# Ordering the small time-mixing work of a two-layer encoder: one chain of 36 steps per pair, a new pair every 8 slots

## The chip, the cores and the metric

The kernel runs on one core of one Trainium2 chip. TensorE (PE) multiplies, with its weight loads (PEld) overlapped; VectorE (DVE), ScalarE (ACT) and GpSimd (POOL) do elementwise work; SyncE (SP) issues the transfers. The metric is the device time of one execution in microseconds, smaller is better.

## The reference

The program is a two-layer encoder over 256 tokens of width 2048, in float32, batch 1. Layer 0 is RWKV-7 time mixing and a squared-ReLU MLP, layer 1 is chunked band attention and an MLP; every branch has an RMS norm and a shift, scale and gate computed from a vector `c` (the modulation). The change concerns the time mixing. Cut to what matters:

```python
xr, xw, xk, xv, xa, xg = [h + xx * mu[j] for j in range(6)]
r, k, v = xr @ w_r, xk @ w_k, xv @ w_v
w_log = -softplus(-(w0 + tanh(xw @ w1) @ w2)) - 0.5
a = sigmoid(a0 + (xa @ a1) @ a2)
g = sigmoid(xg @ g1) @ g2
kk = heads(k * k_k); kk = kk / norm(kk)
k = k * (1 + (a - 1) * k_a)
decay = exp(-exp(heads(w_log)))
def step(S, inp):                       # one token, 32 heads of 64x64 state
    sa = einsum('bhvk,bhk->bhv', S, -kk_t)
    S = S * w_t + sa[..., None] * (kk_t * a_t) + v_t[..., None] * k_t
    return S, einsum('bhvk,bhk->bhv', S, r_t)
y = group_norm(scan(step)) + sum(r * k * r_k) * v
return (y * g) @ w_o
```

## The kernel before, in words

Activations lie transposed: 128 channels (two heads, a *pair*) on the partitions, 256 tokens along the free axis, 16 pairs. Large products split each float32 operand into a high and a low part: a weight half of 128 x 1024 is fetched (`raw`), its high part is made by ScalarE (`wH`, line 371), the low one by VectorE (`wL`, line 374), and `proj2` multiplies each block of 128 rows twice, with 512 columns (line 405) and with 256 (line 406).

The scan is not run token by token but in four chunks of 64 tokens per pair. `Pair` holds it, as generators that yield at the end of every step. `early` (8 steps) makes decays, normalised keys and the scaled operands `kr`, `bh`, `kh`; `invert` (12 steps that do work) makes the 64 x 64 Gram matrices (PSUM tile `gr`) and inverts their triangular part by doubling, in 32 x 32 tiles (`iv`, `tt`, `xs`, `u`); `late` (16 steps) walks through the chunks. For each chunk c it forms `g` (read from PSUM by ScalarE), then `sa` (again ScalarE), then the state update, which VectorE adds to the old state as `zs` (lines 295 and 297). The three stand in the PSUM tile `chn`. The chunk's outputs are added up by further matmuls into the tile `py` (lines 283, 286, 301). After the chunks come the group norm, the gate and the product with `lg`.

Around the pairs, `proj_steps` makes k and r of a pair in 16 large steps of four matmuls (two blocks of rows each), and `out_steps` begins the output projection, in 44 large steps, once the last pair is projected. The modulation is summed on VectorE, one `raw` tile of 128 x 1024 per step (`ada`, lines 445 and 447).

The order: `layer_a` runs 19 periods of 16 slots. In period p, pair p is projected, pair p - 1 is in `early`, p - 2 in `invert`, p - 3 in `late`, each spread evenly over the 16 slots. In each slot the small steps are traced, then one large step; large work is queued on TensorE behind the small work of the slot before, and otherwise the scheduler of the language orders each engine's instructions from what it expects of readiness. `fin` gives out the column sums of the modulation a few at a time, and `ADA_SLOTS` names the slots with a modulation step. Each engine takes its instructions in the order so fixed.

PSUM has eight banks: two `pj` (large products), two `ms` (small ones), and one each of `gr`, `iv`, `chn` and `py`. `reuse_waits="tile"` pools make the next user of a buffer wait for the last readers of the old one. The lines on which the change turns:

```python
pch = pp.tile([P, 3, C], F32, tag="chn", bufs=1, name="chn")
nc.tensor.matmul(pch[K, 2, :], bk[K, 0, c, :], sa[K, :], start=False, stop=True)
nc.vector.scalar_tensor_tensor(out=zn, in0=zs, scalar=pc[:, c, :], in1=pch[:, 2, :], ...)
nc.tensor.matmul(ch(py)[K, c, :], sa[K, :], ch(ar)[K, c, :], start=False, stop=True)
```

Of the kernel before, what the change touches and what calls it, by code (L numbers as in the profile page):

```python
# [18 lines left out]
P = 128  # L19
D = 2048  # L20
T = 256
# [56 lines left out]
class Pair:  # L78

    EARLY = 8

    def __init__(self, body, j, v, tw, ta, tg, e01):
        self.b, self.j, self.v, self.tw, self.ta, self.tg, self.e01 = body, j, v, tw, ta, tg, e01
        self.heads = (slice(0, C), slice(C, P))

    def s(self, name="s", bufs=10):
        return self.b.pw.tile([P, T], F32, tag=name, bufs=bufs, name=name)
# [28 lines left out]
    def early(self):  # L118
# [27 lines left out]
        self.pc = pw.tile([P, 4, 1], F32, tag="pc", bufs=3, name="pc")  # L146
# [18 lines left out]
        kr = self.kr = self.big("kr", 3)  # L165
# [3 lines left out]
        rkp = s("rkp", 1)  # L169
# [4 lines left out]

        bk = self.bk = pw.tile([P, 3, 4, C], F32, tag="bk", bufs=3, name="bk")
        pt = b.psm().rearrange("p (a c k) -> p a c k", a=2, c=4)
        self.each(lambda c: pt[:, 0, c, :], lambda c: ch(v)[:, c, :], lambda c: cst("cen"))
        nc.scalar.copy(bk[:, 2], pt[:, 0])
# [5 lines left out]

    def invert(self):
        b, nc, s, ch, kr, bk, bh, kh = self.b, self.b.nc, self.s, self.ch, self.kr, self.bk, self.bh, self.kh
# [5 lines left out]
        def half(name, bufs):  # L192
            return b.pw.tile([P, 4, H], F32, tag=name, bufs=bufs, name=name)
# [10 lines left out]
        ar = self.ar = s("ar", 2)  # L204
# [20 lines left out]
        nc.scalar.copy(bk[:, 0:2], pt)  # L225
# [3 lines left out]
        for l in range(1, 6):  # L229
            tt_, xs = half("tt", 1), half("xs", 1)  # L230
            nc.vector.transpose(out=tt_.rearrange("p c t -> p (c t)"), in_=u.rearrange("p c t -> p (c t)"))
            pi = pp.tile([P, 16, H], F32, tag="iv", bufs=1, name="iv")[:, 0:4, :]
# [10 lines left out]
            pi = pp.tile([P, 16, H], F32, tag="iv", bufs=1, name="iv")[:, 0:4, :]  # L243
            if l < 5:
                self.tiles(pi, xs, u, [(i, i) for i in range(4)])
                nc.vector.tensor_tensor(out=u, in0=u, in1=pi, op=ALU.add)
            else:
                self.tiles(pi, xs, u, up)
                for K in QS[::2]:
                    nc.vector.tensor_copy(uf[K, :, H:C], pi[K])  # L250
            if l == 2:
                pg = pp.tile([P, 4, P], F32, tag="gr", bufs=1, name="gr")
                self.each(lambda c: pg[:, c, :], lambda c: ch(kh)[:, c, :], lambda c: kr[:, c, :])
                mk = self.mk = self.big("mk", 2)
                nc.vector.tensor_tensor(out=mk, in0=pg, in1=ui, op=ALU.mult)
            yield

    def late(self):
        b, nc, j, s, ch, v = self.b, self.b.nc, self.j, self.s, self.ch, self.v
        kr, ar, mk, bk, u, pc, heads = self.kr, self.ar, self.mk, self.bk, self.u, self.pc, self.heads  # L260
        pw, pp = b.pw, b.pp

        pyt = pp.tile([P, 2, T], F32, tag="py", bufs=1, name="py")
        py = pyt[:, 0, :]
        zs = None
        for c in range(4):
            if c == 1:
                lg = pw.tile([P, 2, P], F32, tag="lg", bufs=1, name="lg")
                nc.sync.dma_start(out=lg, in_=b.d["lora2"][j, :, 2:4])
            pch = pp.tile([P, 3, C], F32, tag="chn", bufs=1, name="chn")  # L270
            g, sa = (pw.tile([P, C], F32, tag=n_, bufs=2, name=n_) for n_ in ("g", "sa"))
            for K in heads:
                nc.tensor.matmul(pch[K, 0, :], mk[K, c, 0:C], bk[K, 2, c, :], start=True, stop=(c == 0))  # L273
            if c:
                for K in heads:
                    nc.tensor.matmul(pch[K, 0, :], kr[K, c, 0:C], zs[K, :], start=False, stop=True)
            nc.scalar.copy(g, pch[:, 0, :])
            yield
            for K in heads:
                nc.tensor.matmul(pch[K, 1, :], u[K, c, :], g[K, :], start=True, stop=True)  # L280
            nc.scalar.mul(sa, pch[:, 1, :], -1.0)
            for K in heads:
                nc.tensor.matmul(ch(py)[K, c, :], bk[K, 2, c, :], mk[K, c, C:P], start=True, stop=False)
            if c:
                for K in heads:
                    nc.tensor.matmul(ch(py)[K, c, :], zs[K, :], kr[K, c, C:P], start=False, stop=False)
            yield
            if c < 3:
                for K in heads:
                    nc.tensor.matmul(pch[K, 2, :], bk[K, 1, c, :], bk[K, 2, c, :], start=True, stop=False)  # L290
                for K in heads:
                    nc.tensor.matmul(pch[K, 2, :], bk[K, 0, c, :], sa[K, :], start=False, stop=True)
                zn = pw.tile([P, C], F32, tag="zs", bufs=2, name="zs")
                if c == 0:
                    nc.vector.tensor_copy(zn, pch[:, 2, :])
                else:
                    nc.vector.scalar_tensor_tensor(out=zn, in0=zs, scalar=pc[:, c, :], in1=pch[:, 2, :],
                                                   op0=ALU.mult, op1=ALU.add)
                zs = zn
            for K in heads:  # L300
                nc.tensor.matmul(ch(py)[K, c, :], sa[K, :], ch(ar)[K, c, :], start=False, stop=True)
            yield

        var, pg = pyt[:, 1, :], pyt[:, 1, :]
        sq = self.square(py)
        yield
        self.head_sums(var, sq)
        yield
        rg = s("sl", 2)
# [3 lines left out]
        yield  # L313
        for i in range(2):
            nc.tensor.matmul(pg, lg[:, i, :], self.tg[:, i, :], start=(i == 0), stop=(i == 1))  # L315
# [5 lines left out]
class Body:  # L321
    RAW_BUFS = 6
    W_BUFS = 3
    DRAIN_STEPS = (14, 14, 16)
    ADA_SLOTS = (1, 3, 6, 9, 11, 14)
    ADA_MORE = 10
# [296 lines left out]
    def layer_a(self, st, sp):  # L623
# [184 lines left out]
        with ExitStack() as s1:  # L808
# [12 lines left out]
            def proj_steps(pr):  # L821
                pr.lw = pw.tile([96, 2, P], F32, tag="lw", bufs=2, name="lw")
                nc.sync.dma_start(out=pr.lw, in_=d["lora2"][pr.j, :96, 0:2])
                for dst, hl in (("k", xk), ("r", xr)):
# [4 lines left out]
                    for kt in range(KT):  # L829
                        self.proj2(ps, w, lambda kt: hl[:, kt, :, 0:T], (kt, kt + 1))  # L830
                        if kt % 2 == 1:
# [7 lines left out]
            def out_steps():  # L839
# [3 lines left out]
                sums, todo = self.o_ps, [(n, 0, HK) for n in range(4)] + [(n, HK, KT - 2) for n in range(4)]  # L843
                for n, lo, hi in todo + [(n, 0, HK) for n in range(4, 8)]:
# [4 lines left out]
                    if lo == HK and n == 0:  # L849
                        for j in range(HK, KT - 2):  # L850
                            self.split(self.y_hl, j, v[:, j, :])
# [7 lines left out]
            stages = ((Pair.late, 16), (Pair.invert, 13), (Pair.early, Pair.EARLY), (None, 16))  # L859
            smalls, larges = [], []  # L860
            for p in range(NPAIR + 3):
                live = []
                if p == NPAIR:
                    self.y_hl = self.new_hl()
                    outs = out_steps()
                for i, (f, n) in enumerate(stages):
                    j = p - 3 + i
                    if 0 <= j < NPAIR:
                        live.append([proj_steps(pairs[j]) if f is None else f(pairs[j]), n, 0])
                if p >= NPAIR:  # L870
                    live.append([outs, self.DRAIN_STEPS[p - NPAIR], 0])
                dense = live.pop()
                for slot in range(16):

                    for gens, own, other, back in ((live, smalls, larges, 0), ([dense], larges, smalls, 2)):
                        with tc.issue_after(other[-back]) if back and len(other) >= back else nullcontext():
                            for g in gens:
                                while g[2] * 16 < g[1] * (slot + 1):
                                    next(g[0], None)
                                    g[2] += 1  # L880
                        own.append(self.last_pe())
                    self.lazy = True
                    self.fin(2)
                    if p >= 2 and (slot in self.ADA_SLOTS or slot == 7 and 3 <= p < 3 + self.ADA_MORE):
                        self.ada()
                    self.lazy = False
# [307 lines left out]
```

## Time and profile before

| | |
|---|---|
| median of 3 runs | 2713.09 us |
| lowest, highest | 2711.19, 2715.17 us |
| span of the profiled execution | 2707.4 us |
| between the span and the runs' times | 3.8 to 7.8 us (median 5.7) |
| pairs' stage, first large matmul to last small step | 210.3 to 750.3 us |
| TensorE busy, share of the span | 2645.1 us, 98% |
| VectorE busy | 2104.9 us, 78% |
| ScalarE busy | 1347.8 us, 50% |
| DMA, mean | 245 GB/s |

The profile is that of one execution; the page gives its span, from the first to the last instruction, and not its whole time, so sums are made against the span. A row of a group has the line, the engine, the operation, the tile written and the tiles read, the shapes and the count. A small float32 matmul shows twice in the trace, so "x4" in a row of a 64 x 64 product is one for each of the two heads. Matmuls are pipelined and their ends are modelled: times between two matmuls are best taken from start to start. "PE a <- DVE b" in the list of waits means that TensorE's instruction a stood idle until VectorE's b had ended.

### The profile page before, as it was taken

How to read it: one execution, taken by the hardware profiler on the slowest of the kernel's cores; microseconds unless marked ns; L12 is line 12 of the kernel's file. 1: busy time of each engine (PE TensorE's matmuls, PEld its weight loads, DVE VectorE, ACT ScalarE, POOL GpSimd, SP SyncE). 2: the span in 40 equal slices, each digit the busy share in tenths (PEclk: the TensorE clock that was granted, in tenths of full speed). 3: DMA queues.
4: the chain of work that ended last, by engine and by line, in shares of the span. 5: the costliest groups of instructions: out<-in, count | busy, mean ns of one | idle time of the engine just before them, and what ended most of it. 6: DMA issues, size and time to landing. Idle time of an engine off the chain costs nothing.

```text
span 2707.4 us, 58382 instructions
## 1 busy us (share of the span) xinstructions
PE 2645.1 (98%) x23690; PEld 2236.3 (83%) x23690; DVE 2104.9 (78%) x3109; ACT 1347.8 (50%) x2432; POOL 214.9 (8%) x320
## 2 busy tenths in 40 slices
PE   6999999999999999999999999999999999999997
PEld 3777777777888888888888898877898888888886
DVE  5778888888788788888888898899987555555555
ACT  3346444555355536445355554465565464453553
POOL 0002222322110000000000100000100000000002
PEclk9999999999999999999999999999999999999999
DMA  9966655665587789988889769887867555555553
GB/s 338 313 227 207 203 191 180 191 195 177 184 280 264 255 324 329 330 307 319 322 316 329 252 220 316 322 287 252 288 193 259 188 188 186 187 188 186 189 188 120
DMA packets 217390, 662.64 MB, mean 245 GB/s; under 512 B 21408, under 2 KB 68896, under 8 KB 217120
## 3 DMA queue, kind: packets, MB, share of 16 engines
q1 hardware_dynamic: 215056, 656.36, 71.7%
q8 instruction: 186, 3.05, 0.4%
q10 hardware_dynamic: 2064, 2.54, 0.3%
q14 instruction: 84, 0.69, 0.1%
HBM read 656.72 MB, written 2.10 MB: 243 GB/s over the span
## 4 chain that ended last, share of the span: by engine, by line
PE 91%; DVE 3%; issue 3%; ACT 1%; DMA 1%; POOL 1%; DVEq 0%; ACTq 0%; SPq 0%; POOLq 0%
PE pj L405 47%; PE pj L406 23%; PE iv L107 2%; PE pj L395 2%; PE pj L396 2%; PE pj L394 2%; PE gr L101 1%; PE o L394 1%; PE ms L101 1%; PE chn L273 1%; PE chn L280 1%; PE ms L111 1%; PE py L315 1%; DVE wL L374 1%; PE o L395 0%
## 5 line engine op out<-in xcount | busy, mean ns | idle before, releaser
L374 DVE TENSOR_TENSOR wL<-raw,wH 128x1024 fp32r<-128x1024 f32 x772 | 941.8, 1220 | 353.5 <-ACT wH L371 348.8
L405 PE MATMUL pj<-aHL,wH 128*128 128x512 f32 x3328 | 1214.3, 405 | 2.0 <-DVE x L914 1.1
L371 ACT CAST wH<-raw 128x1024 fp32r<-128x1024 f32 x772 | 805.9, 1045 | 796.6 <-PE pj L405 650.4
L406 PE MATMUL pj<-aHL,wL 128*128 128x256 f32 x3328 | 938.8, 282 | 0.0
L405 PEld LDWEIGHTS pj<-aHL,wH 128*128 128x128 f32 x3328 | 628.0, 189 | 154.4 <-issue 11.4
L405 PE MATMUL pj<-hHL,wH 128*128 128x512 f32 x2048 | 722.4, 398 | 0.0
L406 PEld LDWEIGHTS pj<-aHL,wL 128*128 128x128 f32 x3328 | 628.3, 189 | 3.9 <-issue 0.8
L406 PE MATMUL pj<-hHL,wL 128*128 128x256 f32 x2048 | 574.4, 281 | 0.0
L405 PEld LDWEIGHTS pj<-hHL,wH 128*128 128x128 f32 x2048 | 384.5, 188 | 93.8 <-DVE hHL L960 0.2
L406 PEld LDWEIGHTS pj<-hHL,wL 128*128 128x128 f32 x2048 | 386.8, 189 | 0.5 <-DVE wL L374 0.3
L447 DVE SCALAR_TENSOR_TENSOR acc<-rada,ct,acc 128x1024 f32<-128x1024 f32 x255 | 326.3, 1280 | 11.7 <-DMA rada<-w_ada 11.1
L511 POOL TENSOR_TENSOR ss<-ss,sq 128x256 f32<-128x256 f32 x56 | 54.8, 979 | 1587.1 <-ACT sq L510 1586.9
L985 DVE SCALAR_TENSOR_TENSOR x<-pj,mod,x 128x256 f32<-128x256 f32 x256 | 123.4, 482 | 58.4 <-PE pj L406 54.6
L447 DVE SCALAR_TENSOR_TENSOR acc<-raw,ct,acc 128x1024 f32<-128x1024 f32 x105 | 135.6, 1291 | 3.8 <-DMA raw<-w_ada 3.7
L396 PE MATMUL pj<-aHL,wL 128*128 128x258 f32 x384 | 108.6, 283 | 1.6 <-DVE wL L374 1.6
L957 ACT ACTIVATE t<-t 128x256 f32<-128x256 f32 x112 | 46.8, 418 | 126.9 <-DVE t L929 126.9
L395 PE MATMUL pj<-aHL,wH 128*128 128x258 f32 x384 | 109.6, 286 | 0.0
L394 PE MATMUL pj<-aHL,wH 128*128 128x258 f32 x384 | 109.5, 285 | 0.0
L396 PEld LDWEIGHTS pj<-aHL,wL 128*128 128x128 f32 x384 | 73.9, 193 | 1.9 <-DVE wL L374 1.8
L395 PEld LDWEIGHTS pj<-aHL,wH 128*128 128x128 f32 x384 | 73.3, 191 | 0.1
L394 PEld LDWEIGHTS pj<-aHL,wH 128*128 128x128 f32 x384 | 73.0, 190 | 0.2
L959 ACT ACTIVATE t<-t 128x256 f32<-128x256 f32 x128 | 53.4, 417 | 3.4
(244 smaller groups left out, 2846.6 us busy)
## 6 DMA issues: line engine op xcount, KB each, us to landing
raw<-w_up SPq DMA_DIRECT2D x256, 512.0 KB, 4.3
raw<-w_down SPq DMA_DIRECT2D x256, 512.0 KB, 4.2
rada<-w_ada SPq DMA_DIRECT2D x208, 512.0 KB, 5.7
raw<-w_ada SPq DMA_DIRECT2D x112, 512.0 KB, 4.4
rawa<-w_ada SPq DMA_DIRECT2D x64, 512.0 KB, 6.7
rada<-w_ada_kv SPq DMA_DIRECT2D x64, 512.0 KB, 6.2
raw<-w_k SPq DMA_DIRECT2D x32, 512.0 KB, 4.7
raw<-w_r SPq DMA_DIRECT2D x32, 512.0 KB, 4.7
```

The source lines that it names most:

```text
L101: self.b.nc.tensor.matmul(o(c)[K], lhsT(c)[K], rhs(c)[K], start=True, stop=True)
L107: self.b.nc.tensor.matmul(o[QS[K], c, :], lhsT[QS[R], c, :], rhs[QS[R], c, :], start=True, stop=True, tile_position=(H * R, H * K))
L371: nc.scalar.copy(Hf, raw)
L374: eng.tensor_tensor(out=Lf, in0=raw, in1=Hf, op=ALU.subtract)
L394: nc.tensor.matmul(ps, H[:, i, :], a(kt)[:, 0, :], start=(first and kt == 0), stop=False)
L395: nc.tensor.matmul(ps, H[:, i, :], a(kt)[:, 1, :], start=False, stop=False)
L396: ins = nc.tensor.matmul(ps, L[:, i, :], a(kt)[:, 0, :], start=False, stop=(last and kt == KT - 1))
L405: nc.tensor.matmul(ps, H[:, i, :], a(kt), start=(kt == 0), stop=False)
L406: ins = nc.tensor.matmul(ps[:, 0, :], L[:, i, :], a(kt)[:, 0, :], start=False, stop=(kt == KT - 1))
L447: nc.vector.scalar_tensor_tensor(out=self.acc, in0=raw, scalar=ck, in1=self.acc, op0=ALU.mult, op1=ALU.add)
L511: (eng or nc.gpsimd).tensor_tensor(out=self.ss, in0=self.ss, in1=sq, op=ALU.add)
L985: nc.vector.scalar_tensor_tensor(out=x, in0=ps[:, i, :], scalar=self.mods[(layer, 5)][:, n:n + 1], in1=x, op0=ALU.mult, op1=ALU.add)
```

## The change

The 36 steps of a pair (8 early, 12 invert, 16 late) become one chain, `Pair.steps`. A slot advances every live pair by exactly one step, and a new pair enters every 8 slots (`SLOTS`), so that four to five pairs are live. Within a slot the pairs come by the kind of their tiles: invert (32 x 32), then late (64 x 64), then early, the older first, each step queued on TensorE behind the one before; then two large steps (four blocks of rows, eight matmuls), and in three of four slots one modulation step, whose column sums are no longer given out piecemeal. The drain after the last projection has 36 slots, with the 44 large steps spread over them; its `todo` list takes the lower halves of all eight output blocks first.

In the late steps `chn` and `py` become one bank, `lt`, with two buffers, so that two pairs can be in `late`; the sums `var` and `pg` and the last inversion level go to the `ms` banks. The output sums of a chunk are now all traced after `zs` and queued behind the state update's matmuls. Buffers are resized to the longer life of what they hold, v's centred transpose gets a tile of its own (`vp`, before it was the third part of `bk`), `lw` gets one buffer and is fetched later, and `lg` is fetched two chunks later. The diff, cut:

```diff
 class Pair:
-    EARLY = 8
+    EARLY, INVERT, LATE = 8, 12, 16
+    STEPS = EARLY + INVERT + LATE
+    def steps(self):
+        yield from self.early()
+        yield from self.invert()
+        yield from self.late()
...
-    def s(self, name="s", bufs=10):
+    def s(self, name="s", bufs=8):
...
+    def corner(self, l):
+        t = self.b.psm() if l == 5 else self.b.pp.tile([P, 512], F32, tag="iv", bufs=1, name="iv")
+        return t.rearrange("p (c t) -> p c t", t=H)[:, 0:4, :]
...
     def late(self):
-        pyt = pp.tile([P, 2, T], F32, tag="py", bufs=1, name="py")
-        py = pyt[:, 0, :]
+        bank = pp.tile([P, 2, T], F32, tag="lt", bufs=2, name="lt")
+        pch, py = bank[:, 0, 0:3 * C].rearrange("p (a t) -> p a t", a=3), bank[:, 1, :]
...
-            if c == 1:
+            if c == 3:
                 lg = pw.tile([P, 2, P], F32, tag="lg", bufs=1, name="lg")
                 nc.sync.dma_start(out=lg, in_=b.d["lora2"][j, :, 2:4])
-            pch = pp.tile([P, 3, C], F32, tag="chn", bufs=1, name="chn")
...
-            for K in heads:
-                nc.tensor.matmul(ch(py)[K, c, :], bk[K, 2, c, :], mk[K, c, C:P], start=True, stop=False)
-            if c:
-                for K in heads:
-                    nc.tensor.matmul(ch(py)[K, c, :], zs[K, :], kr[K, c, C:P], start=False, stop=False)
             yield
+            old = zs
             if c < 3:
                 for K in heads:
-                    nc.tensor.matmul(pch[K, 2, :], bk[K, 1, c, :], bk[K, 2, c, :], start=True, stop=False)
+                    mm(pch[K, 2, :], bk[K, 1, c, :], vp[K, c, :], start=True, stop=False)
                 for K in heads:
-                    nc.tensor.matmul(pch[K, 2, :], bk[K, 0, c, :], sa[K, :], start=False, stop=True)
-                zn = pw.tile([P, C], F32, tag="zs", bufs=2, name="zs")
+                    ins = mm(pch[K, 2, :], bk[K, 0, c, :], sa[K, :], start=False, stop=True)
+                zs = pw.tile([P, C], F32, tag="zs", bufs=4, name="zs")
...
-            for K in heads:
-                nc.tensor.matmul(ch(py)[K, c, :], sa[K, :], ch(ar)[K, c, :], start=False, stop=True)
+            with b.tc.issue_after(ins.ins) if c < 3 else nullcontext():
+                for K in heads:
+                    mm(ch(py)[K, c, :], vp[K, c, :], mk[K, c, C:P], start=True, stop=False)
+                if c:
+                    for K in heads:
+                        mm(ch(py)[K, c, :], old[K, :], kr[K, c, C:P], start=False, stop=False)
+                for K in heads:
+                    mm(ch(py)[K, c, :], sa[K, :], ch(ar)[K, c, :], start=False, stop=True)
             yield
...
+            for slot in range(S * NPAIR + Pair.STEPS):
                 live = []
...
+                for j, pr in enumerate(pairs):
+                    at = slot - S * (j + 1)
+                    if 0 <= at < Pair.STEPS:
+                        if at == 0:
+                            pr.gen = pr.steps()
+                        live.append((0 if at in inverts else 1 + (at < Pair.EARLY), -at, pr))
+                        pr.done = at == Pair.STEPS - 1
+                last = self.last_pe()
+                for _, _, pr in sorted(live, key=lambda x: x[:2]):
+                    with tc.issue_after(last):
+                        next(pr.gen)
+                    last = self.last_pe()
+                if slot < S * NPAIR:
+                    if slot % S == 0:
+                        dense = proj_steps(pairs[slot // S])
+                    todo = 16 // S
...
+                    todo = OUTS * (slot + 1 - S * NPAIR) // Pair.STEPS - n_out
+                    n_out += todo
+                with tc.issue_after(last):
+                    for _ in range(todo):
+                        next(dense, None)
+                if slot >= 2 * S and slot % 4 < 3:
+                    self.ada()
```

More of the change, by code (lines that the diff above doesn't have):

```diff
@@ L842, in out_steps @@
                     self.split(self.y_hl, n, v[:, n, :])
[L843 to L844 removed]
+                sums, todo = self.o_ps, [(n, 0, HK) for n in range(8)] + [(n, HK, KT - 2) for n in range(4)]
+                for n, lo, hi in todo:
                     if n % 2 == 0 and lo == 0:
@@ L849, in out_steps @@
                     if lo == HK and n == 0:
+                        assert all(p.done for p in pairs[:KT - 2])
                         for j in range(HK, KT - 2):
@@ L858, in layer_a @@
             self.o_ps = []
-            stages = ((Pair.late, 16), (Pair.invert, 13), (Pair.early, Pair.EARLY), (None, 16))
-            smalls, larges = [], []
-            for p in range(NPAIR + 3):
+            S, OUTS = self.SLOTS, 44
+            inverts = range(Pair.EARLY, Pair.EARLY + Pair.INVERT)
+            outs, done, n_out = None, 0, 0
+            for slot in range(S * NPAIR + Pair.STEPS):
                 live = []
[L863 to L886, printed above, removed]
```

64 lines of the change are left out of this document (34 added, 30 removed).

## The prediction

> **What bounds the kernel now.** I read the page's busy shares first, then the busy time of the stage that the change touches, then who waits for whom there. The first two rows are the page's span and busy shares; TensorE (PE) is busy 98% of the span, so the question is how full it is in the stage of the pairs.
>
> ```profile
> span 2707.4 us, 58382 instructions
> PE 2645.1 (98%) x23690; PEld 2236.3 (83%) x23690; DVE 2104.9 (78%) x3109; ACT 1347.8 (50%) x2432; POOL 214.9 (8%) x320
> ```
>
> The next rows are busy times by stretch: start and end, length, busy us and instructions of PE, PEld, DVE, ACT and POOL, then the granted clock and the DMA's share and GB/s. The pairs' stage runs from the first large matmul at 210.3 us to the last small step at 750.3; the output projection then runs to 811.7. The stretch from 668.5 to 750.3 is the drain, after the last pair's projection.
>
> ```profile
> 210.30:811.70 601.40, 592.92 (x10017) 468.41 (x10018) 498.47 (x875) 304.73 (x787) 146.83 (x191) 1.00 0.62 201
> 247.00:668.50 421.50, 417.81 (x7877) 317.74 (x7876) 354.12 (x652) 212.25 (x583) 112.39 (x149) 1.00 0.60 193
> 668.50:750.30 81.80, 78.59 (x1457) 66.55 (x1456) 54.67 (x95) 31.16 (x87) 13.10 (x17) 0.98 0.52 166
> 750.30:811.70 61.40, 60.46 (x379) 53.95 (x378) 56.37 (x70) 34.81 (x55) 12.35 (x13) 1.00 0.87 298
> ```
>
> TensorE is idle for 8.5 us of 601.4, VectorE (DVE) is busy 83%. The list of waits in the same stretch says the same (who waited, for whom, us in total, times, longest):
>
> ```profile
> PE iv L107 <- DVE tt L231: 2.2, 4, 0.6
> PE iv L107 <- DVE zs L295: 2.0, 2, 1.4
> PE chn L273 <- DVE zs L295: 1.3, 2, 0.7
> PE py L301 <- issue: 1.0, 1, 1.0
> PE pj L405 <- DVE v L752: 0.9, 1, 0.9
> ```
>
> So TensorE is the bound of the stage, by its own work and not by waiting: a change of its order pays by what it takes off that work, and costs by each wait that it adds to the in-order stream.
>
> **What a small run between large ones costs.** The timeline of one slot (start, length, engine, line, operation) shows the price of going from large matmuls to small tiles and back:
>
> ```profile
> 434.08 0.28 PE L286 MATMUL py<-kr,zs 64*64 64x64 f32 x4
> 434.30 0.50 PE L405 MATMUL pj<-aHL,wH 128*128 128x512 f32 x1
> ...
> 438.01 0.51 PE L405 MATMUL pj<-aHL,wH 128*128 128x512 f32 x1
> 438.35 0.28 PE L406 MATMUL pj<-aHL,wL 128*128 128x256 f32 x1
> 438.47 0.40 PE L405 MATMUL pj<-aHL,wH 128*128 128x512 f32 x1
> 438.71 0.28 PE L406 MATMUL pj<-aHL,wL 128*128 128x256 f32 x1
> ...
> 439.41 0.28 PE L406 MATMUL pj<-aHL,wL 128*128 128x256 f32 x1
> 439.62 0.33 PE L273 MATMUL chn<-bk,mk 64*64 64x64 f32 x4
> 439.78 0.28 PE L276 MATMUL chn<-zs,kr 64*64 64x64 f32 x4
> 439.90 0.28 PE L283 MATMUL py<-mk,bk 64*64 64x64 f32 x4
> ```
>
> From start to start: the first large matmul behind a small group takes 0.34 us (438.01 to 438.35), the next one 0.24 (438.47 to 438.71), so entering costs 0.10. A group of four small ones takes 0.12 when small ones follow (439.78 to 439.90) and 0.22 when a large one follows (434.08 to 434.30), another 0.10. A large 256-column one takes 0.12 inside a run (438.35 to 438.47) and 0.21 ahead of small ones (439.41 to 439.62), 0.09. A round trip costs about 0.29 us, in which nothing is computed.
>
> **The change part by part.**
>
> *Order of the slots.* In the order in which the built programs hand matmuls to TensorE, from the first large matmul of the stage to the first one of the MLP, a run on the whole 128-row array is entered from smaller tiles 287 times before and 173 times after: two large steps per slot stand together, and the 64-wide work of a slot stands together. Changes between 64-wide and 32-wide tiles are 114 before and 109 after, no difference worth counting. 287 - 173 = 114 round trips at 0.29 us take off 33 us. The matmuls themselves are the same; one step of the modulation sums fewer (111 for 112) falls into the stage, and is done later.
>
> *The late chain.* Before, the state update ends in its own bank (chn), and the output sums stand in another (py): the py matmuls that follow in the stream need no answer from VectorE. Afterwards both lie in one tile, lt, and the py matmuls are queued right behind the update. In the built program the first of them (mk, vp) waits, in all 48 cases where there is an update (16 pairs, c = 0, 1, 2), for the zs instruction on VectorE that reads the update just finished. Between the two nothing stands on TensorE. So 48 times the stream stops for a full answer: TensorE's result, VectorE's queue, zs, and back. Behind it wait the other late pair, the early pair and the slot's four large steps. Before, zs was also awaited, but one slot later. What the answer takes is in the trace of before, where VectorE is free and where it isn't:
>
> ```profile
> 404.42 0.28 PE L292 MATMUL chn<-sa,bk 64*64 64x64 f32 x4
> 404.54 0.28 PE L301 MATMUL py<-ar,sa 64*64 64x64 f32 x4
> 404.84 0.28 DVE L297 SCALAR_TENSOR_TENSOR zs<-zs,pc,chn 128x64 f32<-128x64 f32 x1 [0.59 <-PE chn L292]
> ```
>
> ```profile
> 328.40 0.28 PE L292 MATMUL chn<-sa,bk 64*64 64x64 f32 x4
> 328.52 0.28 PE L301 MATMUL py<-ar,sa 64*64 64x64 f32 x4
> 328.84 1.27 DVE L447 SCALAR_TENSOR_TENSOR acc<-raw,ct,acc 128x1024 f32<-128x1024 f32 x1
> 330.03 0.21 DVE L295 COPY zs<-chn 128x64 f32<-128x64 f32 x1
> ```
>
> ```profile
> 674.19 0.19 DVE L295 COPY zs<-chn 128x64 f32<-128x64 f32 x1
> 674.41 0.45 PE L107 MATMUL iv<-tt,al 32*32 32x32 f32 x32 [1.38 <-DVE zs L295]
> ```
>
> The last pair of rows gives the restart: 674.41 - 674.38 = 0.03 us. Free: 404.84 + 0.28 + 0.03 - 404.54 = 0.61 us later than py starts now. Behind an accumulation: 330.03 + 0.21 + 0.03 - 328.52 = 1.75 us. How often which, by the instructions that sat idle until the update was ready:
>
> ```profile
>   DVE zs L297: 12.2, 16
>   DVE zs L295: 0.8, 1
> ```
>
> 17 of 48 found VectorE idle and pay 0.61. The other 31 found it working; I take the middle of both ends for them, 1.18. The mean is (17 x 0.61 + 31 x 1.18) / 48 = 0.98 us, the sum 47 us, between 29 (all free) and 84 (all behind a large one). I don't take the lower end, because VectorE has the same 498 us of work as now, and because in the built order of VectorE two of a pair's three zs stand behind large work of other steps (four early ones; an accumulation or a weight half).
>
> The wait goes by the whole bank, not by the addresses (zs reads columns that py does not write). The Trainium skill, PSUM — Partial Sum Buffer, section "PSUM bank collisions raise a hardware error", asks for just this: guard by bank and quadrant, "not by address". By that rule the 47 us are due; by a guard that goes by addresses they would not be, and the sum would be -33. The built waits follow the rule; no run here shows the chip without them.
>
> *Steps in a fixed order, one per slot.* A pair's step now has the length of a slot to be answered: the first and last large-rank product of the pairs give the present pace,
>
> ```profile
> L123 PE MATMUL ms<-tw,lw x32: 377/380/484, 221.6 to 668.8; 96*128 96x256 f32 x32
> ```
>
> (668.8 - 221.6) / 15 = 29.8 us per pair, 1.9 us per slot of 16, 3.7 per slot of 8. Late and invert steps get more time than now, early ones about the same (8 steps in 8 slots for 8 in 16). The waits that TensorE has now, 8.5 us, may go or stay: I leave them. If this cover fails, an in-order stream pays each miss in full, as for zs.
>
> *Buffers.* bk without its third part, vp of its own, s with 8 for 10 and rkp in it, tt, xs, g, sa, zs, kr, mk, ar one or two more: no instruction more or less. The s buffers come back at least a slot before they are needed. The sums var and pg and the last inversion level move to the two ms banks, which then get about 9 uses per 8 slots; their readers are one slot back. I cost this at nothing; if a reader is late, the price is that of an operation in front of it on VectorE, up to 1.3 us a pair.
>
> *SyncE's queue.* lw has one buffer for two and is fetched in the pair's fourth slot, when its last reader has long run, four slots (15 us) ahead of use; lg is fetched two late steps later, two slots after its last reader and six ahead of its use. A weight transfer of 512 KB behind them lands in under 5 us:
>
> ```profile
> raw<-w_k SPq DMA_DIRECT2D x32, 512.0 KB, 4.7
> ```
>
> lg can hold back the transfers behind it to two slots (7 us) before they are used: hidden, by 2 us.
>
> *Drain.* 36 slots for 48, with 44 steps of the output projection as before, and more small work (four and a half pairs for three) and 27 modulation steps for 18. This is moved work and not new; 11 of the 48 stalls lie there.
>
> Sum: -33 + 47 = +14 us, and the bounds -33 + 29 = -4 and -33 + 84 = +51. Against the profiled span 2707.4 that is 2721; the runs' median, 2713.09, lies 5.7 above that span, so I forecast 2727.
>
> **The rivals.**
>
> *Faster: VectorE answers at once.* Place: the same 48 waits. If zs is always taken first, each costs 0.61, and the 8.5 us of waits that TensorE has now are swallowed by them, since the other chains get that time as well: -33 + 29 - 9 = -13, 2700. It decides below 33 / 48 = 0.69 us per stall. For it: 17 of 48 found VectorE idle, and TensorE's own pauses let VectorE catch up. Against: 83% busy, and zs has no precedence in the queue. A variant in which the wait is covered wholly gives -33, 2680; against it stands the built order.
>
> *Even.* Stalls of 0.6 to 0.8 us without that swallowing: within 5 us of the median, 2713.
>
> *Much slower: zs mostly stands behind an accumulation or a weight half.* 1.75 each: +51, 2764. For it: the built order of VectorE. Against: VectorE goes on working during each stall, so its backlog cannot grow to that at every one.
>
> *The clock.* Stops inside the stage may lower the granted clock. The stretch ahead of it, in which TensorE is idle for 14%, shows 0.98:
>
> ```profile
> 0.00:226.00 226.00, 194.38 (x1658) 147.24 (x1659) 156.16 (x327) 89.56 (x154) 13.53 (x22) 0.98 0.85 283
> ```
>
> 2% of the stage's 560 us would be another 11 us: +25, 2738. The Trainium skill, TensorE: Matmul & The Clock Gate, section "A second HAM failure mode: psum-queue depth-cycling", tells of such a throttle where TensorE pauses between groups. The stretch quoted bears it out at most by 0.02, with longer pauses than one microsecond, so it gets little.
>
> *The change doesn't do what it says.* The built order has two large steps together in nearly every slot, so this gets no share.
>
> **How the numbers follow.** Forecast (stalls of 0.85 to 1.4): 0.50. Even: 0.15. Faster by quick answers: 0.15, by no stall at all: 0.06. Much slower: 0.10. Clock: 0.04. A measurement of this kernel tells 0.2%, 5.4 us, from no change. So faster 0.21, same 0.15, slower 0.64. The range reaches from a little under the quick-answer case, 2695, to the much slower one, 2763; outside lie the case without a stall and half of the worst one and some tail, under 0.2. The likeliest case alone spans -33 + 41 to -33 + 67, 2721 to 2747.
>
> **What the profile afterwards would show.** Right: in the waits of TensorE, lt behind zs near 48 times and 30 to 60 us in total; large runs of eight matmuls with one slow first one; the last product of the pairs (ms from tw) near or a little after 668 us; VectorE's busy time of the stage near 498. Wrong, faster: that wait in sum under 30 us, the last product clearly before 650. Wrong, slower: other waits of TensorE of the same size, such as iv behind tt or ms behind its readers, or a granted clock under 0.99 in the stage. I would be wrong above all if the round trip's 0.29 us does not fall with the number of runs, or if VectorE's queue stands differently when zs is due.

## The result, and the profile after

The changed kernel takes 2724.38 us (median of 4 runs, 2722.68 to 2725.98), the kernel before, run beside it, 2714.13: the ratio is 1.0046, with a 95% interval of 1.0034 to 1.0058. It is slower by 0.46%. The forecast was 2727.0.

The page's span and busy shares of the changed kernel, to be set beside those of before (2707.4 us, PE 2645.1):

```profile
span 2721.4 us, 58341 instructions
PE 2614.4 (96%) x23690; PEld 2233.9 (82%) x23690; DVE 2104.5 (77%) x3109; ACT 1345.5 (49%) x2432; POOL 200.1 (7%) x320
```

TensorE does the same 23,690 matmuls in 31 us less, and the span is 14.0 us longer. Busy times by stretch (columns as in the prediction) of the stage, of its middle and of its drain:

```profile
211.30:832.80 621.50, 563.45 (x9952) 467.34 (x9953) 490.77 (x867) 301.80 (x787) 132.77 (x192) 0.98 0.59 192
247.00:681.90 434.90, 390.77 (x7810) 317.37 (x7810) 339.93 (x633) 206.21 (x575) 100.02 (x148) 0.97 0.54 173
681.90:770.00 88.10, 80.13 (x1540) 68.26 (x1536) 68.75 (x117) 35.55 (x100) 13.35 (x21) 0.98 0.64 215
```

The stage is 621.5 us long in place of 601.4. TensorE's busy time in it fell by 29.5 (592.9 to 563.4), its idle time rose by 49.5 (8.5 to 58.0). The granted clock, 1.00 before, is 0.98. What it waits for in the stage (us in total, times, longest):

```profile
PE lt L304 <- DVE zs L300: 30.2, 29, 3.3
PE lt L304 <- DVE zs L298: 12.6, 15, 2.1
PE iv L111 <- DVE tt L239: 10.5, 9, 4.5
```

The first two rows are the waits that the prediction named: 44 of them, 42.8 us. The third was 2.2 us before. The timeline shows one such wait of 1.99 us, from the update (line 295) on, and behind it the start of the run of eight large matmuls with one slow first one (302.25 to 302.59 is 0.34; the next of its kind, 302.70 to 302.94, takes 0.24):

```profile
298.93 1.17 DVE L227 TENSOR_TENSOR u<-u,csts 128x128 f32<-128x128 f32 x1 [1.18 <-POOL u L221]
299.48 0.28 PE L295 MATMUL lt<-sa,bk 64*64 64x64 f32 x4
300.02 0.27 DVE L254 TENSOR_TENSOR u<-u,iv 128x128 f32<-128x128 f32 x1
300.33 0.51 DVE L239 STREAM_TRANSPOSE tt<-u 128x128 f32<-128x128 f32 x2
300.76 0.77 DVE L145 TENSOR_TENSOR_SCAN s<-csts,s 128x256 f32<-128x256 f32 x1
301.45 0.25 DVE L300 SCALAR_TENSOR_TENSOR zs<-zs,pc,lt 128x64 f32<-128x64 f32 x1
301.75 0.33 PE L304 MATMUL lt<-mk,vp 64*64 64x64 f32 x4 [1.99 <-DVE zs L300]
302.03 0.28 PE L309 MATMUL lt<-ar,sa 64*64 64x64 f32 x4
302.25 0.50 PE L412 MATMUL pj<-aHL,wH 128*128 128x512 f32 x1
302.59 0.28 PE L413 MATMUL pj<-aHL,wL 128*128 128x256 f32 x1
302.70 0.40 PE L412 MATMUL pj<-aHL,wH 128*128 128x512 f32 x1
302.94 0.28 PE L413 MATMUL pj<-aHL,wL 128*128 128x256 f32 x1
```

zs was late here because VectorE was still at work on u for the inverse steps (until 300.29) and then did two transposes for them and a scan for the early pair, all small work of the pairs.

Such a stop costs a little more than its idle time. The profile lets idle time begin at the modelled end of the update (299.48 + 0.28 = 299.76), while in an unbroken stream the next group starts 0.12 us behind it (404.42 to 404.54 in the prediction). The other 0.16 us of each stop is counted as busy: 44 x 0.16 = 7.0 us.

Behind the stage, 7.1 us came back: from its end to the span's end it was 2707.4 - 811.7 = 1895.7 before, and is 2721.4 - 832.8 = 1888.6. Before, the start of the MLP held these two waits, which are gone:

```profile
L396 PE MATMUL pj<-aHL,wL 128*128 128x258 f32 x128 | 36.6, 288 | 1.6 <-DVE wL L374 1.6
L516 PE MATMUL m<-ss,csts 128*128 128x256 f32 x2 | 0.7, 431 | 4.0 <-DVE ss L511 4.0
```

Ahead of the stage it is 1.0 us more (210.3 to 211.3). In sum: 1.0 - 29.5 + 49.5 - 7.1 = +13.9 us, against 14.0 between the spans.

### The profile page after: what moved, and what is told of

Read it like the earlier page. It is cut to its first block, busy times and chain, and to the rows that moved or that the text cites. A ratio compares the mean times of both kernels' runs of the same rounds, so it can differ in the third digit from the quotient of the medians.

```text
span 2721.4 us, 58341 instructions
## 1 busy us (share of the span) xinstructions
PE 2614.4 (96%) x23690; PEld 2233.9 (82%) x23690; DVE 2104.5 (77%) x3109; ACT 1345.5 (49%) x2432; POOL 200.1 (7%) x320
## 4 chain that ended last, share of the span: by engine, by line
PE 69%; DVE 1%; DMA 1%; issue 0%; ACT 0%; DVEq 0%; ACTq 0%; SPq 0%
PE pj L412 41%; PE pj L413 21%; PE pj L402 2%; PE pj L401 2%; PE pj L403 2%; DMA rada<-w_ada 1%; PE m L476 0%; PE pT L1102 0%; DVE acc L454 0%; PE po L1109 0%; DVE wL L381 0%; PE S L1081 0%; PE o L401 0%; PE S L1080 0%; PE o L403 0%; PE o L402 0%
## 5 line engine op out<-in xcount | busy, mean ns | idle before, releaser
L454 DVE SCALAR_TENSOR_TENSOR acc<-raw,ct,acc 128x1024 f32<-128x1024 f32 x104 | 136.7, 1315 | 27.3 <-DMA raw<-w_ada 27.0
L970 ACT ACTIVATE t<-t 128x256 f32<-128x256 f32 x112 | 46.8, 418 | 122.9 <-DVE t L942 122.9
L304 PE MATMUL lt<-mk,vp 64*64 64x64 f32 x256 | 21.9, 247 | 42.8 <-DVE zs L300 30.2
```

What stands on the lines that cost most here:

```text
L304: mm(ch(py)[K, c, :], vp[K, c, :], mk[K, c, C:P], start=True, stop=False)
L454: nc.vector.scalar_tensor_tensor(out=self.acc, in0=raw, scalar=ck, in1=self.acc, op0=ALU.mult, op1=ALU.add)
L970: nc.scalar.activation(t, t, AF.Relu)
```

## The experiments

Each ratio is to the kernel before on the same chip (medians of 2710 to 2711 us), with its 95% interval. "Stage" is as above, from the first large matmul of the pairs to the first one of the MLP.

### The same change without the stall

The output sums of chunk c move from right behind their state update to the head of the pair's next late step, one slot later. Everything else stays.

```
+        def outputs(c, old, sa):  # the three groups of py matmuls, as they were
...
         for c in range(4):
+            if c:
+                outputs(*held)
...
-            with b.tc.issue_after(ins.ins) if c < 3 else nullcontext():
-                (the py matmuls)
+            held = c, old, sa
+            if c == 3:
+                outputs(*held)
             yield
```

> The changed kernel, with a chunk's output sums (py) queued one slot later, at the head of the pair's next late step, so that in the built order mostly 20 to 44 matmuls stand between the state update and the first instruction that waits for zs; nothing else is changed. Theory A, the 48 answers of VectorE cost what the trace shows (42.8 us of TensorE idle in front of lt<-mk,vp): 2724 - 43 = 2681 us; and if the half-clock stretches of the stage (31 us of them afterwards, 3 before) come from these pauses, up to 13 us less, 2668. The wait lt behind zs goes to under 5 us in total. Rival B, VectorE's queue bounds the stage and the wait moves on: iv behind tt rises from 10 us to 30 or more, and the time stays above 2705 us.

Measured: 2678.89 us, ratio 0.9877 (0.9860 to 0.9894). The waits of lt for zs fell from 42.8 us to 1.5:

```profile
L111 PE MATMUL iv<-tt,al 32*32 32x32 f32 x2048 | 30.3, 195 | 10.3 <-DVE tt L239 10.0
...
L275 PE MATMUL lt<-mk,vp 64*64 64x64 f32 x256 | 19.9, 232 | 1.5 <-DVE zs L309 0.8 <-DVE zs L311 0.6
```

That is theory A. The stage's row (columns as above) is

```profile
211.44:788.84 577.40, 548.25 (x9953) 458.56 (x9953) 489.87 (x867) 300.74 (x787) 142.38 (x192) 0.99 0.64 207
```

So the place of the output sums costs 45 us, and the rest of the change is worth 32 us to the good. That 45 is close to the 42.8 us of waits for zs is in part chance. In the stage, idle time is 29.1 us in place of 58.0: the waits for zs fell by 41, but other waits rose from 15.2 to 27.7, so some of the waiting did move on, as rival B had it. Busy time is 548.2 in place of 563.4: the time at half clock is 13.7 us in place of 30.7, worth 8.5, and the other 6.7 fit the 7.0 that the stops had put into busy time. This version beats both kernels.

### The shared bank alone

The kernel before, with its own order of steps, takes over the late part of the change: state update and output sums in one tile lt, the py matmuls queued behind the update.

```
-        pyt = pp.tile([P, 2, T], F32, tag="py", bufs=1, name="py")
+        bank = pp.tile([P, 2, T], F32, tag="lt", bufs=2, name="lt")
+        pch, py = bank[:, 0, 0:3 * C].rearrange("p (a t) -> p a t", a=3), bank[:, 1, :]
...
+            with b.tc.issue_after(ins.ins) if c < 3 else nullcontext():
+                (the py matmuls, behind the update)
```

> The kernel before, with the late steps of the change alone (update and outputs in one bank, var and pg in the small banks, outputs traced behind zs), in the old order of 19 periods of 16 slots, where the scheduler may place other work between: in the built order 3 to 37 matmuls stand between the update and the first output in all 48 cases. Theory A, what costs is the answer with nothing between: 2714 to 2726 us, the waits lt behind zs under 15 us. Rival B, the shared bank costs by itself: 2714 + 43 = 2757 us.

Measured: 2713.18 us, ratio 1.0009 (0.9993 to 1.0025): not told apart from the kernel before, theory A. In this built order 3 to 37 other matmuls stand between the update and the first output sum, and the waits for zs stay small:

```profile
PE iv L107 <- DVE zs L291: 4.1, 3, 1.6
PE lt L297 <- DVE zs L291: 2.3, 4, 0.8
```

The shared bank makes the wait due, but it costs only where nothing stands in between. The Trainium skill, PSUM — Partial Sum Buffer, section "PSUM bank collisions raise a hardware error", asks for a guard by bank and not by address; the built waits follow it, and what these runs add is its price: 42.8 us of idle time in the changed kernel, where the writer comes next, 2.3 here, where other work does.

### Slots half as long

In the version without the stall, 16 slots a pair in place of 8, one large step each, so that the runs on the whole array are short again.

```
-    SLOTS = 8
+    SLOTS = 16
...
-                if slot >= 2 * S and slot % 4 < 3:
+                if slot >= 2 * S and slot % 7 < 3:
```

> As e1, with a new pair every 16 slots and one large step per slot, the modulation steps thinned to 3 of 7 slots so that their number stays. Large runs are entered 265 times instead of 173. Theory A, a round trip between large and small tiles costs 0.29 us: 92 x 0.29 = 27 us slower than e1. Rival B, the number of runs doesn't matter: within 6 us of e1.

Measured: 2809.3 us, ratio 1.0357 (1.0341 to 1.0372), far more than either theory gave. The waits of the stage:

```profile
PE iv L111 <- DVE tt L239: 51.2, 25, 3.9
PE ms L111 <- DVE tt L239: 8.8, 10, 1.7
```

A slot half as long no longer covers the answers that a step needs from VectorE: idle time is 94.4 us, and 95.6 us of the stage ran at half clock. The time therefore doesn't give the price of an entry. The busy time does so roughly. With half of what was busy at half clock taken off, it is 611.3 - 87.2 / 2 = 567.7 us here and 548.2 - 11.9 / 2 = 542.3 in the version without the stall. The 25 us between them are 0.28 for each of the 92 entries, at most, as there are more stops here and each has its busy part. Here one step per slot worked only while a slot outlasted an answer.

### No modulation steps beside the updates

In the changed kernel the modulation steps go to slots in which no pair updates its state.

```
-                if slot >= 2 * S and slot % 4 < 3:
+                if slot >= 2 * S and slot % 8 in (0, 2, 3, 5, 7):
```

> The changed kernel, with the modulation steps (1.3 us each on VectorE) in 5 of 8 slots, none in the three in which zs falls due, so that 92 of 111 fall in the stage and the rest later. Theory A, 0.61 us of a stall is the round trip and the rest is VectorE's queue: the waits lt behind zs fall from 43 to about 30 us, and the time to about 2711 us. Rival B, other work of VectorE stands in front of zs instead: 43 us, 2724 us.

Measured: 2750.4 us, ratio 1.0141 (1.0125 to 1.0156), which neither theory gave. The waits for zs did not shrink:

```profile
PE lt L304 <- DVE zs L300: 33.2, 30, 3.2
PE lt L304 <- DVE zs L298: 16.8, 16, 2.6
```

The edit moved the steps to other slots, but VectorE often comes to them only in the next one: by the trace, in 15 of the 25 slow answers an accumulation is still at work between the update and zs, where it was 9 of 22 without this edit. So the run doesn't separate the two theories. The time from the stage's end on rose from 1888.6 to 1913.1 us, because 19 modulation steps fell out of the stage and into the MLP, where TensorE then waits for weight halves (up to 5.7 us per kind of wait). That is a cost of the edit and not of the stall.

### One large step between the inverse and the late steps

This run asks for the price of entering a run on the whole array. In the version without the stall, one of the slot's two large steps is put ahead of the late and early steps.

```
+                cut = False
+                for kind, _, pr in sorted(live, key=lambda x: x[:2]):
+                    if kind and not cut and slot < S * NPAIR:
+                        with tc.issue_after(last):
+                            next(dense, None)
+                        last, cut = self.last_pe(), True
```

> The kernel with output sums one slot later (2679), with one edit: of the two large steps of a slot, one goes in between the slot's invert step and its late and early steps. Slots, waits and all instructions stay; in the built order the runs on the whole array are entered 252 times in place of 173, and changes between 32- and 64-wide tiles fall from 109 to 56. Theory A (a run on the whole array has a price, which is what the change saves): 79 entries at 0.29 are 23 us, at 0.44 35 us, less up to 6 for the 53 changes, so 2696 to 2714, with TensorE's busy time in the stage 17 to 35 us above 548. Theory B (the entries are free and the stage became quicker for another reason, its fixed order): 2679 within 5, and busy time as it was. If waits come and go with the new place, they show as idle time and not as busy time.

Measured: 2675.78 us, ratio 0.9867 (0.9852 to 0.9881), not told apart from 0.9877. By the time, theory B; by the busy time, theory A or a little under it (17 to 35 us more were expected). The stage's row, to be set beside the one of the version without the stall, is

```profile
210.16:787.54 577.38, 564.09 (x9952) 455.01 (x9953) 488.13 (x867) 302.72 (x787) 132.42 (x192) 0.99 0.64 207
```

Busy time rose by 15.8 us, and idle time fell by the same 15.8 (29.1 to 13.3), since the inverse steps' answers now have a large step to hide behind:

```profile
PE iv L111 <- DVE tt L239: 4.1, 6, 1.1
```

Entries do have a price. The half-clock time of the stage went from 13.7 us to 6.8, which is worth 3.4 us of busy time the other way, so the 79 entries less the 53 changes of tile width cost 19.2 us at full clock. That is 0.24 an entry if the changes of width are free. At 0.29 an entry it would be 23, which leaves 4 us, 0.07 each, for the changes of width.

### One modulation step less before

The kernel before had 112 modulation steps in the stage, the changed one 111. Here the kernel before has 111.

```
-    ADA_MORE = 10
+    ADA_MORE = 9
```

> The kernel before with one modulation step less inside the stage (ADA_MORE 9: 111 steps in place of 112, the same number as the changed kernel has there); the step left out runs later. Theory A (the 4.0 us wait of TensorE for the sum of squares at the start of the MLP, and 1.6 for a weight split, come from VectorE being behind with that last step): the waits go, 2704 to 2708. Theory B (they come from the old order at the end of the stage): 2711 to 2713, and the 4.0 us wait stays.

Measured: 2704.96 us, ratio 0.9978 (0.9968 to 0.9989): 5.8 us faster, theory A. The wait of 4.0 us is gone:

```profile
L516 PE MATMUL m<-ss,csts 128*128 128x256 f32 x2 | 0.6, 380 | 0.0
```

The trace puts 4.2 of the 5.8 us behind the stage (1891.5 us from its end on, in place of 1895.7) and 1.9 into the stage. So some 4 of the 7 us that the change gained behind the stage go with this one step that it no longer had room for, and not with its new order; the other 3 stay open.

### VectorE's large work behind zs

In the changed kernel, VectorE's part of the two large steps and of the modulation step may come in its queue only behind the slot's zs.

```
+                held, self.zi = self.zi, None  # self.zi: the slot's zs instruction
-                with tc.issue_after(last):
+                with tc.issue_after(last), tc.issue_after(held) if held else nullcontext():
                     for _ in range(todo):
                         next(dense, None)
-                if slot >= 2 * S and slot % 4 < 3:
-                    self.ada()
+                    if slot >= 2 * S and slot % 4 < 3:
+                        self.ada()
```

> The changed kernel with one edit: in each slot that updates the state, VectorE's part of the two large steps and the modulation step may be put in its queue only behind that slot's update of zs. Theory A (a part of the stall is VectorE finishing other work before it answers: longest 3.3 us where the free answer takes 0.61): the waits of lt for zs fall from 43 us to 48 times 0.61, some 30, and with fewer half-clock windows the time to 2700 to 2713. Theory B (VectorE's place in its queue is not it, or the work only moves in front of another answer): 2724 within 5, with the 43 us there or moved to other waits.

Measured: 2719.17 us, ratio 1.0034 (1.0017 to 1.0050): 5 us under the changed kernel by the medians, 3 by the two ratios, whose intervals overlap, so no gain is shown. The waits of the stage:

```profile
PE lt L304 <- DVE zs L300: 25.8, 32, 1.9
PE lt L304 <- DVE zs L298: 17.1, 16, 1.5
PE iv L111 <- DVE tt L239: 4.4, 5, 1.8
```

The long waits are gone (1.9 us in place of 3.3), but the sum is the same 43 us, now in all 48 cases, at 0.90 each: theory B. By the trace 23 of the 48 restarts come within 0.70 us of the update, as free answers do. 12 zs still stand behind a scan on a tile s, such as the one above. Of the other 13, 9 stand behind a weight half of an earlier slot, which the edit doesn't hold back, and which itself waits for ScalarE first:

```profile
338.76 1.04 ACT L378 CAST wH<-raw 128x1024 fp32r<-128x1024 f32 x1 [1.24 <-PE pj L412]
339.44 0.28 PE L295 MATMUL lt<-sa,bk 64*64 64x64 f32 x4
339.84 1.23 DVE L381 TENSOR_TENSOR wL<-raw,wH 128x1024 fp32r<-128x1024 f32 x1 [1.27 <-ACT wH L378]
340.98 0.22 DVE L298 COPY zs<-lt 128x64 f32<-128x64 f32 x1
341.25 0.33 PE L304 MATMUL lt<-mk,vp 64*64 64x64 f32 x4 [1.53 <-DVE zs L298]
```

So this run doesn't test an empty queue. What one would leave can be estimated: the 23 free answers still cost 0.38 to 0.47 us of idle time each, which for 48 is 18 to 23 us. So a shorter queue could take off about half of this stall; work between update and output sum took off nearly all of it. What did change beside the long waits: iv behind tt 10.5 to 4.4, and half-clock time 30.7 to 13.7 us.

### The same edit where nobody waits for zs

The last two runs put that edit on top of the version without the stall, and on top of the one with the split large steps, where the second large step and the modulation step are held back:

```
+                held, self.zi = self.zi, None
-                with tc.issue_after(last):
+                with tc.issue_after(last), tc.issue_after(held) if held else nullcontext():
```

> The kernel with output sums one slot later (2679) with the edit that puts VectorE's large work of a slot behind that slot's update of zs. There are no waits of lt for zs left to shorten; what is left is 10.0 us of inverse steps that wait for the transpose tt, 13.7 us at half clock and 11 us of other waits. Theory A (the large work stands in front of the small answers, tt as well): idle time falls from 29 to about 20 and the time to 2662 to 2674. Theory B (the place behind zs matters only where the next matmul waits for zs): 2679 within 5.

Measured: 2697.0 us, ratio 0.9942 (0.9926 to 0.9957).

> The kernel with one large step between the inverse and the late steps (2676) with the same edit for the second large step and the modulation step. Idle time in its stage is 13.3 us. Theory A: idle time and the last half-clock window shrink, 2667 to 2673. Theory B: 2676 within 5.

Measured: 2734.4 us, ratio 1.0082 (1.0064 to 1.0099). Both theories missed in both runs: the edit costs 18 and 59 us. In the first run TensorE now waits for the large work that came late, for weight halves (3.3 us before this edit) and for modulation sums (none before):

```profile
PE o L409 <- DVE wL L387: 7.2, 6, 2.1
PE ms L482 <- DVE acc L460: 5.8, 5, 1.7
```

In the second run VectorE itself waits (first row), and TensorE's inverse steps wait for VectorE (second):

```profile
DVE zs L309 <- PE lt L306: 22.6, 8, 3.3
```

```profile
PE iv L111 <- DVE tt L239: 30.7, 16, 3.2
```

An order that is forced in an in-order queue is a wait for that queue too. In the second run VectorE sits idle until zs's input is there. That it then does its large work late and meets the next slot's small answers with it fits the waits of both runs, but was not tested by itself.

## Why the prediction was right, and which terms were not

The sum was -33 + 47 = +14 us, and the spans differ by +14.0. The direction and the mechanism were right: fewer runs take work off TensorE, and the stops of the late chain cost more than that. That the sum was hit to the microsecond is luck. TensorE's busy time fell by 29.5. Without the 13.7 that the clock added to it (half of the 27.3 us more at half clock, below) and the 7.0 that the stops added, it fell by 50.2. The measured terms are then: 1.0 ahead of the stage, -50.2 for the order of the slots, +13.7 for the clock, +49.8 for zs (42.8 idle and 7.0 busy), +6.7 other waits (58.0 - 42.8 - 8.5), -7.1 behind the stage; in sum 13.9.

*The late chain (+47).* Right in place and number, and its size is within 3 us: 42.8 us of idle time in 44 waits, 49.8 with the busy part, where the prediction counted how much later py starts, 48 times 0.98. The mix was another one. 17 answers at 0.61 and 31 at 1.18 were forecast; measured by the same start-to-start rule, 20 took 0.60 on average and 22 took 1.68. The prediction said that nothing stood between update and output sum in all 48 cases; by the trace part of a modulation sum stands there in the other 6, and these cost next to nothing. Fewer slow answers, each slower, gave the same sum. What made them slow was not only accumulations and weight halves: some stood behind small work alone, such as the one shown above. That the place of the output sums is the cause of the stall is shown by the run that moved only them (-45 us).

*The order of the slots (-33).* This is the term that was mis-sized: 50 us, where 114 x 0.29 = 33 was forecast. The version without the stall, which enters as often as the changed kernel, says the same without the 7.0: its busy time without the clock's part, reckoned as above with half of the time at half clock, is 541.4 against 591.2 before, 49.8 less. The price of 0.29 itself roughly holds: the rows shown from the changed kernel have 0.34 and 0.24 again, and the runs with 79 and 92 entries more give 0.24 and at most 0.28 an entry. So the new order saved some 17 us that entries don't explain, and what they are stays open. A part may lie in the 64-wide matmuls: from the start of one to the start of the next 64-wide one it is 35.9 ns on average before and 31.4 in the version without the stall, which for some 2,200 of them is about 10 us, an estimate.

*The clock.* It had a chance of 0.04, at +11 us, as a rival; it came, beside the forecast case and not in place of it. The stage's mean granted clock fell from 1.00 to 0.98, with 30.7 us at half clock in place of 3.4, which is worth 27.3 / 2 = 13.7 us, or 12.4 if only the 28.1 us of it are counted in which TensorE was busy. The rival's size was right and its chance too small: a forecast that adds stops of up to 3 us to a stage had to add the clock to its sum. A granted clock under 0.99 in the stage was also one of its own signs of being wrong, and it showed. The Trainium skill, TensorE: Matmul & The Clock Gate, section "A second HAM failure mode: psum-queue depth-cycling", tells of short pauses between groups that bring the throttle back; the trace agrees, with 30.7 us.

*Steps in a fixed order.* The 8.5 us of waits were "left"; waits other than those for zs are 15.2 us, most of it iv behind tt (10.5 for 2.2). A step of the inverse chain is answered late where large VectorE work is in front. In the half-long slots (51.2 us) an accumulation or a weight half was in front in most of the long cases, and in many VectorE had itself waited for GpSimd.

*The modulation step that is done later.* The prediction saw it and gave it no price. In the kernel before it was worth 5.8 us, most of it at the start of the MLP, as the run with 111 steps shows.

*Buffers, SyncE's queue.* TensorE waits 0.9 us in all, twice, for a reader of the two ms banks and never for lw or lg: next to nothing, as forecast. *Drain:* 88.1 us for 81.8 in the rows, with 80.1 busy for 78.6; most of the difference is waits. The last product of the pairs starts at 682.3, a little after 668 as was said, and VectorE's busy time in the stage is 490.8 (498 was said; the missing modulation step's part is in that).

So +14 was hit because the misses cancel: runs -17.2 and behind the stage -7.1 on the one side, clock +13.7, other waits +6.7, zs +2.8 and the start +1.0 on the other, in sum -0.1.

*Of the rivals,* the quick answer (0.61 each) held for 20 of the waits but not for the mean. "No stall at all" (2680) is what the change becomes when its output sums come a slot later: 2678.89 was measured.

## What to carry to other kernels

Putting work of a kind together on TensorE pays by the entry, here about 0.24 to 0.29 us each by the rows and the two runs that added entries; but in a fixed in-order stream look at each matmul that shares a bank with a result another engine has yet to read, and put other work in between, here one slot (45 us of a 2700 us kernel). Price a stop three times: its idle time, the 0.16 us that the profile books as busy, and the clock if the stop is long. Before ordering an engine's queue by hand, ask what that engine will wait for: the same edit was worth 5 us at most where the waiting matmul came next, and cost 18 and 59 where it didn't. And when a sum comes out to the microsecond, check its terms one by one all the same.

## What the hardware showed that I had not expected

A single stop of 1.5 to 3 us was enough here to halve the clock for 3.4 us. These rows (length, then PE busy; the clock is third from the end) are three stretches in a row of the changed kernel, 3.41 us each. Time at half clock comes in such pieces in these traces, or in whole multiples of them, so they are called windows here:

```profile
413.51:416.92 3.41, 1.65 (x28) 1.49 (x29) 2.90 (x4) 0.37 (x2) 0.00 (x0) 1.00 0.89 204
416.92:420.33 3.41, 3.41 (x59) 2.69 (x58) 1.88 (x3) 0.49 (x2) 0.00 (x0) 0.50 0.78 273
420.33:423.75 3.42, 3.42 (x62) 2.91 (x62) 1.25 (x2) 1.88 (x5) 0.00 (x0) 1.00 0.74 297
```

TensorE is idle for 1.76 us of the first, in a wait for zs of 2.1 us that begins a little ahead of it; the clock is half for the whole of the second, in which TensorE is busy throughout, and full again in the third. Eight stretches of the changed kernel's stage were like this, one of them two windows long. The window ahead of each had 1.46 to 2.96 us of idle time, and nearly all of that lay in one stop: a wait for zs in seven cases, in the eighth the longest wait for tt (4.5). Short stops did not add up to the same: of the windows that no half clock followed, all but three had at most 1.35 us of idle time, and the most was 1.68. In the version without the stall there were three such stretches, after 1.62 to 3.15 us. With VectorE's large work behind zs, 48 stops of the same total but of at most 1.9 us gave four such stretches, 13.7 us in place of 30.7. It is no sharp threshold: there 1.46 us was enough once and 1.79 was not, and the one half-clock window of the kernel before came after 0.73. The Trainium skill, TensorE: Matmul & The Clock Gate, section "HAM oscillation — how this bites in real kernels", tells of idle gaps longer than about 3.4 us; here a stop of less than half of that, within one window, was enough.
